# Seven half-size products in place of eight for the first layer's output projection

## The chip, the cores and the metric

The kernel runs on one core of a Trainium2 chip. TensorE (PE in the profile) multiplies matrices into PSUM banks; VectorE (DVE), ScalarE (ACT) and GpSimd (POOL) do the element-wise work; 16 DMA engines move data between HBM and the on-chip memory (SBUF). Transfers are issued from queues, here that of SyncE (SP) and, in the change, that of POOL. The metric is the device time of one execution in microseconds (us), as the median of several runs.

## The reference

A two-layer decoder trunk on 512 tokens of width 1024, in float32. The first layer is a pooling mixer, the second a latent attention; a final RMSNorm follows. What matters here is the end of the first layer and what comes next:

```python
def pool_layer(x, norm_g, w_in, w_group, scale, w_out):
    ...
    mixed = jnp.einsum('bsgc,gcd->bsgd', pooled, w_group).reshape(B, S, POOL_WIDTH) * scale
    y = mixed * jax.nn.silu(z)
    return x + y @ w_out          # y: 512 x 2048, w_out: 2048 x 1024
```

Its result is normalised (RMSNorm) and multiplied by `mla_w_in` in the second layer.

## The kernel before

Matrix products keep float32 accuracy with three products of rounded parts. Every operand is split into `hi` (rounded, by an ACT copy) and `lo` (the rest, by a DVE or POOL subtraction), and `mm3` (L181 to L184) adds hi x hi, lo x hi and hi x lo into a PSUM bank. One `mm3` is three matmuls of a 128x128 stationary tile with up to 512 moving columns. `halves` (L186 to L188) is the pair of instructions that splits a tile.

Weights come in strips. `Strip` (L129 to L168) loads pieces of at most 512 columns into five `raw` buffers over SP's queue (L154, L160) and splits them into a hi and a lo tile of 2048 columns (L166, L167). These tiles share the tag `w` with four buffers (`WB`), so two strips are in flight.

The activations `y` (2048 channels in 16 blocks of 128 partitions, times 512 tokens) lie transposed on chip. They are written group by group, four blocks per group, at L523 (`y[:, c, :]`), after the group's matmuls (L511 to L525) that read `d_hi` and `d_lo`. `h_hi` and `h_lo` (L210, L211) hold the split, normalised tokens of the first layer; their last readers are the gate products of the last group (L503 to L510), which come just before that group's matmuls.

The output projection `OutProj` (L528 to L572) accumulates over the 16 channel blocks, two to a strip, into eight PSUM banks: four tiles of 128 tokens times two halves of 512 output columns. A strip needs 2 x 4 x 2 = 16 calls of `mm3`, 48 matmuls; the eight strips make 384. For each strip four weight pieces and two `y` blocks are split. The last strip is worked off tile by tile (`last_block`, L587 to L592): two banks are finished, added to the residual `xs` (`add`, L572), and `norm_a` (L214 to L218) squares the rows on ACT, forms the reciprocal root in two small POOL steps (L202, L203) and scales on DVE (L217). `norm_b` (L220 to L227) transposes the result on TensorE and splits it into `h_hi`/`h_lo`, where the second layer's first products (`lat_block`, L608 to L636) read it. Their weight strips use the same tag `w`, and POOL makes their `lo` parts.

The order in which each engine issues its instructions, and the semaphores between engines, are fixed when the kernel is compiled, by a planner that goes by the order of the code and by when it reckons each instruction's inputs and buffers to be ready; an instruction whose inputs are ready earlier can be put ahead of one that the code has before it. At run time each engine keeps to that order.

Of the kernel before, what the change touches and what calls it, by code (L numbers as in the profile page):

```python
# [11 lines left out]
F32 = mybir.dt.float32  # L12
F32R = mybir.dt.float32r
I32 = mybir.dt.int32
AF = mybir.ActivationFunctionType
ALU = mybir.AluOpType

P = 128
D = 1024
S = 512  # L20
NT = S // P
KD = D // P
W = 2048
# [9 lines left out]
PAD = 16  # L33
SCALE = (DN + DR) ** -0.5
WB = 4
# [15 lines left out]
def trunk_kernel(  # L51
# [17 lines left out]
    nc = tc.nc  # L69
    pe, act, dve, pool = nc.tensor, nc.scalar, nc.vector, nc.gpsimd  # L70

    def f32(ap):
        return ap.bitcast(F32)
# [4 lines left out]
    wp = ctx.enter_context(tc.tile_pool(name="wp", bufs=2))  # L78
# [5 lines left out]
    def open_pool(name, stack, **kw):  # L84
        return stack.enter_context(
            tc.tile_pool(name=name, bufs=1, reuse_waits="tile", **kw)
        )
# [3 lines left out]
    wk = open_pool("wk1", phase)  # L91

    def bank(dtype=F32):
        return ps.tile([P, 512], dtype, name="bank", tag="bank")

    def xn_tile(dtype=F32, width=D):
        return nm.tile([P, width], dtype, name="xn", tag="xn", bufs=2)


    xs = cp.tile([P, NT, D], F32, name="xs")  # L100
# [9 lines left out]
    def row(src, n, name, **kw):  # L110
        t = cp.tile([P, n], F32, name=name, **kw)
        nc.sync.dma_start(t, src.partition_broadcast(P))
        return t
# [15 lines left out]
    class Strip:  # L129


        def __init__(self, parts, cuts=1, small=False):
            width, kw = (WS, dict(tag="ws", bufs=2)) if small else (W, dict(tag="w", bufs=WB))
            self.hi = wp.tile([P, width], F32R, name="w_hi", **kw)
            self.lo = wp.tile([P, width], F32R, name="w_lo", **kw)
            self.views, self.pieces, at = [], [], 0
            for src, a, c in parts:
                hi, lo = (
                    t[:, at : at + a * c].rearrange("p (a c) -> p a c", a=a)
                    for t in (self.hi, self.lo)  # L140
                )
                self.views.append((hi, lo))
                at += a * c
                w = min(c // cuts, RC)
                g = min(a, RC // w)
                if len(src.shape) == 4:
                    g = 1
                for c0 in range(0, c, w):
                    for a0 in range(0, a, g):
                        n = min(g, a - a0)  # L150
                        raw = wp.tile([P, RC], F32, name="raw", tag="raw", bufs=RB)
                        raw = raw[:, : n * w]
                        if len(src.shape) == 4:
                            nc.sync.dma_start(  # L154
                                raw.rearrange("p (m c) -> p m c", m=src.shape[2]), src[:, a0]
                            )
                            raw = raw.rearrange("p (a c) -> p a c", a=n)
                        else:
                            raw = raw.rearrange("p (a c) -> p a c", a=n)
                            nc.sync.dma_start(raw, src[:, a0 : a0 + n, c0 : c0 + w])  # L160
                        i = (slice(None), slice(a0, a0 + n), slice(c0, c0 + w))
                        self.pieces.append((raw, hi[i], lo[i]))
# [7 lines left out]
    def strip(parts, eng=dve, small=False):  # L170
        st = Strip(parts, small=small)
        st.split(st.pieces, eng)
        return st.views
# [4 lines left out]
    def w_rows(w, k0, k):  # L178
        return w[k0 * P : (k0 + k) * P, :].rearrange("(k p) c -> p k c", p=P)

    def mm3(o, a, b, start, stop):  # L181
        pe.matmul(o, a[0], b[0], start=start, stop=False)  # L182
        pe.matmul(o, a[1], b[0], start=False, stop=False)  # L183
        pe.matmul(o, a[0], b[1], start=False, stop=stop)  # L184

    def halves(src, hi, lo):  # L186
        act.activation(hi, src, AF.Copy)  # L187
        dve.tensor_tensor(lo, src, f32(hi), ALU.subtract)  # L188
# [17 lines left out]
    def inv_rms(src, junk, n):  # L206
        return rsqrt(sum_sq(src, junk, n))

    y = cp.tile([P, KW, S], F32, name="y")
    h_hi = hp.tile([P, KD, S], F32R, name="h_hi")  # L210
    h_lo = hp.tile([P, KD, S], F32R, name="h_lo")  # L211
    hp.tile([P, 24], F32, name="rim")

    def norm_a(t, g):  # L214
        xn = xn_tile()
        rs = inv_rms(xs[:, t, :], xn, D)
        dve.scalar_tensor_tensor(xn, xs[:, t, :], rs, g, ALU.mult, ALU.mult)  # L217
        return xn  # L218

    def norm_b(t, xn):  # L220
        for b in range(2):
            pt = bank()
            for i in range(4):
                k = 4 * b + i
                pe.transpose(pt[:, i * P : (i + 1) * P], xn[:, k * P : (k + 1) * P], ident)
            o = (slice(None), slice(4 * b, 4 * b + 4), slice(t * P, (t + 1) * P))
            halves(pt.rearrange("p (k c) -> p k c", k=4), h_hi[o], h_lo[o])  # L227

    def hmm(o, wv, ct, cols):
        for k in range(KD):  # L230
            a = tuple(v[:, k, ct * P : (ct + 1) * P] for v in wv)
            b = tuple(v[:, k, cols] for v in (h_hi, h_lo))
            mm3(o[:, cols], a, b, k == 0, k == KD - 1)
# [218 lines left out]
    def branch():  # L452

        u = wk.tile([P, 2, PAD + S], F32, name="u", tag="t4", bufs=4)
        pool.memset(u[:, :, :PAD], 0.0)
        return u

    d_hi = wk.tile([P, 4, S], F32R, name="d_hi")
    d_lo = wk.tile([P, 4, S], F32R, name="d_lo")
# [22 lines left out]
    for g in range(4):  # L482
        pooled_from = []
        if g == 0:
            for j in range(2):
                u = branch()
# [5 lines left out]
            g_mla = row(mla_norm[0], D, "g_mla", tag="gain")  # L492
        else:
            for j in range(2):
                (wv,) = strip([(w_cols(w_in, g * 512 + j * 256, 256), KD, 256)])
                u = branch()
                for i in range(2):
                    b = bank()
# [4 lines left out]
        for j in range(2):  # L503
            (wv,) = strip([(w_cols(w_in, W + g * 512 + j * 256, 256), KD, 256)])
            for i in range(2):
                b = bank()
                hmm(b, wv, i, whole_row)
                z = wk.tile([P, S], F32, name="zs", tag="z", bufs=8)
# [3 lines left out]
        for o in range(4):  # L512
            b = bank()
            for k in range(4):
                mm3(
                    b,
                    tuple(v[:, k, o * P : (o + 1) * P] for v in wv),
                    (d_hi[:, k, :], d_lo[:, k, :]),
                    k == 0,
                    k == 3,  # L520
                )
            c = 4 * g + o
            dve.scalar_tensor_tensor(  # L523
                y[:, c, :], b, gcol[:, GS + c : GS + c + 1], zs[o], ALU.mult, ALU.mult
            )  # L525


    class OutProj:  # L528
# [3 lines left out]
        def load(self, s, tile_of):  # L532
            (wv,) = strip([(w_rows(self.w, 2 * s, 2), 2, D)])
            ys = []
            for j in range(2):
                yh, yl = tile_of("h", j), tile_of("l", j)
                halves(y[:, 2 * s + j, :], yh, yl)
                ys.append((yh, yl))
            self.st[s] = (wv, ys)
# [7 lines left out]
        def block(self, s, t, n, j):  # L547
            wv, ys = self.st[s]
            if (t, n) not in self.acc:
                self.acc[t, n] = bank()  # L550
            mm3(
                self.acc[t, n],
                tuple(v[:, t * P : (t + 1) * P] for v in ys[j]),
                tuple(v[:, j, n * 512 : (n + 1) * 512] for v in wv),
                s == 0 and j == 0,
                j == 1 and s == (6 if self.apart == (t, n) else 7),
            )
# [13 lines left out]
            c = slice(n * 512, (n + 1) * 512)  # L571
            return dve.tensor_tensor(xs[:, t, c], self.acc[t, n], xs[:, t, c], ALU.add)  # L572

    def y_tile(half, j):
        return wk.tile([P, S], F32R, name=f"y{half}", tag="z", bufs=8)


    o1 = OutProj(pool_w_out[0])
    for s in range(8):
        o1.load(s, y_tile)  # L580
        if s < 7:
            for j in range(2):
                for t in range(NT):
                    for n in range(2):
                        o1.block(s, t, n, j)

    def last_block(t):  # L587
        for n in range(2):
            for j in range(2):
                o1.block(7, t, n, j)  # L590
            o1.add(t, n)
        return norm_a(t, g_mla)  # L592

    w_in2 = mla_w_in[0]
    xn = {t: last_block(t) for t in range(2)}
    xn[2] = last_block(2)
    norm_b(0, xn[0])
    xn[3] = last_block(3)
    norm_b(1, xn[1])

    phase.close()
    lT = ExitStack()
# [192 lines left out]
    for i in range(3, 8):  # L795
# [5 lines left out]
    wk = ap = open_pool("wk3", phase)  # L801
# [3 lines left out]
        out=mask[:, 384:],  # L805
# [179 lines left out]
    for h in range(H):  # L985
        p, odd = divmod(h, 2)
        g, t = divmod(h + 5, 4)
# [35 lines left out]
    for s in range(2, 8):  # L1023
# [4 lines left out]
    o = [  # L1028
        ap.tile([P, D], F32, name="o", tag=tag, bufs=n)
        for tag, n in (("pm", 2), ("pm", 2), ("pt_hi", 1), ("pt_lo", 1))  # L1030
    ]
# [113 lines left out]
```

## Time and profile before

| | us |
|---|---|
| median of three runs | 739.25 (738.48 to 739.72) |
| profiled execution, its time | 740.2 |
| profiled execution, its span | 738.2 |
| TensorE busy | 722.7 (98%) |
| VectorE busy | 384.8 (52%) |
| ScalarE busy | 318.9 (43%) |
| GpSimd busy | 96.9 (13%) |

The span runs from the first to the last instruction of the profiled execution; its own time also counts what lies around it. The projection's matmuls start at 234.7 us; its last sums and the norms lie between 312 and 332 us. A line such as `L182 PE MATMUL bank<-w_hi,yh` names the line of the kernel, the engine, the operation, and the tiles written and read; the releaser in brackets is what an engine had waited for before it.

### The profile page before, as it was taken

What the parts mean: (1) busy time and instruction counts of PE and PEld (TensorE: products, weight loads), DVE (VectorE), ACT (ScalarE), POOL (GpSimd) and SP (SyncE); (2) the same over time, 40 slices, a digit from 0 to 9 for tenths busy, and PEclk for the clock granted to TensorE, in tenths of its full rate; (3) what the DMA queues carried; (4) which work ended last, traced back from release to release, by engine and by line L of the source; (5) the groups of instructions that cost most, each with busy time, mean ns of one, the idle gap of its engine ahead of it and who ended that gap; (6) DMA issues with size and microseconds to landing.
All of it is one profiled execution on the core that took longest, in us unless ns stands there. A gap on an engine that the chain in (4) does not pass through costs nothing.

```text
span 738.2 us, 10030 instructions
## 1 busy us (share of the span) xinstructions
PE 722.7 (98%) x3619; PEld 616.8 (84%) x3619; DVE 384.8 (52%) x800; ACT 318.9 (43%) x727; POOL 96.9 (13%) x143
## 2 busy tenths in 40 slices
PE   7999999999999999999999999999999999999995
PEld 6988888888888888889888888898888988888884
DVE  5864454464565333271644311686876877744325
ACT  6452242232333323243652325665566565623314
POOL 5000000000000000153600005221232020000006
PEclk8999999999999999999999999999999999999998
DMA  8342332332233233124333424122132131113203
GB/s 256 106 141 64 108 115 72 100 115 86 85 115 92 80 115 107 43 78 130 95 115 98 131 76 122 51 50 79 51 96 75 31 108 58 57 58 115 83 18 114
DMA packets 61985, 68.09 MB, mean 92 GB/s; under 512 B 11760, under 2 KB 45680, under 8 KB 61936
## 3 DMA queue, kind: packets, MB, share of 16 engines
q1 hardware_dynamic: 61792, 67.26, 30.4%
q8 instruction: 28, 0.46, 0.2%
q10 hardware_dynamic: 144, 0.20, 0.1%
q14 instruction: 21, 0.17, 0.1%
HBM read 61.15 MB, written 2.10 MB: 86 GB/s over the span
## 4 chain that ended last, share of the span: by engine, by line
PE 92%; DVE 4%; ACT 1%; POOL 1%; issue 1%; DMA 0%; POOLq 0%; SPq 0%; ACTq 0%
PE bank L183 28%; PE bank L184 28%; PE bank L182 28%; PE bank L941 2%; PE bank L300 2%; PE bank L904 1%; PE bank L905 1%; DVE xn L217 1%; PE bank L907 1%; ACT pm L927 1%; DVE pm L933 1%; PE bank L270 1%; DVE nm L924 0%; DMA xs<-in_x 0%; ACT xn L197 0%
## 5 line engine op out<-in xcount | busy, mean ns | idle before, releaser
L166 ACT ACTIVATE w_hi<-raw 128x512 fp32r<-128x512 f32 (+2 forms) x240 | 127.3, 584 | 192.3 <-PE bank L183 184.7
L167 DVE TENSOR_TENSOR w_lo<-raw,w_hi 128x512 fp32r<-128x512 f32 x172 | 111.8, 690 | 172.6 <-ACT w_hi L166 172.6
L182 PE MATMUL bank<-h_hi,w_hi 128*128 128x512 f32 x368 | 143.4, 390 | 0.0
L184 PE MATMUL bank<-h_lo,w_hi 128*128 128x512 f32 x368 | 143.2, 389 | 0.0
L183 PE MATMUL bank<-h_hi,w_lo 128*128 128x512 f32 x368 | 143.2, 389 | 0.0
L167 POOL TENSOR_TENSOR w_lo<-raw,w_hi 128x256 fp32r<-128x256 f32 (+2 forms) x68 | 62.2, 945 | 304.7 <-ACT w_hi L166 304.6
L184 PEld LDWEIGHTS bank<-h_lo,w_hi 128*128 128x128 f32 x368 | 69.1, 188 | 14.4
L182 PEld LDWEIGHTS bank<-h_hi,w_hi 128*128 128x128 f32 x368 | 69.1, 188 | 14.3
L183 PEld LDWEIGHTS bank<-h_hi,w_lo 128*128 128x128 f32 x368 | 69.1, 188 | 14.2
L182 PE MATMUL bank<-w_hi,yh 128*128 128x512 f32 x128 | 49.9, 390 | 0.0
L184 PE MATMUL bank<-w_lo,yh 128*128 128x512 f32 x128 | 49.8, 389 | 0.0
L183 PE MATMUL bank<-w_hi,yl 128*128 128x512 f32 x128 | 49.8, 389 | 0.0
L182 PE MATMUL bank<-latT_hi,w_hi 128*128 128x512 f32 x104 | 42.3, 407 | 0.0
L184 PE MATMUL bank<-latT_lo,w_hi 128*128 128x512 f32 x104 | 40.7, 391 | 0.0
L183 PE MATMUL bank<-latT_hi,w_lo 128*128 128x512 f32 x104 | 40.7, 391 | 0.0
L911 DVE CUSTOM_DVE_ANT_0 pm<-bank,mask 128x128 f32<-128x128 f32 (+2 forms) x64 | 30.6, 489 | 16.0 <-PE bank L184 11.0
L927 ACT ACTIVATE pm<-pm,nm 128x128 f32<-128x128 f32 (+1 forms) x64 | 35.3, 557 | 2.4 <-DVE nm L924 2.0
L187 ACT ACTIVATE pt_hi<-bank 128x512 fp32r<-128x512 f32 (+2 forms) x48 | 20.1, 491 | 22.4 <-PE bank L941 22.4
L184 PEld LDWEIGHTS bank<-w_lo,yh 128*128 128x128 f32 x128 | 24.0, 188 | 5.0
L182 PEld LDWEIGHTS bank<-w_hi,yh 128*128 128x128 f32 x128 | 24.0, 188 | 5.0
L183 PEld LDWEIGHTS bank<-w_hi,yl 128*128 128x128 f32 x128 | 24.0, 188 | 4.9
L184 PE MATMUL bank<-d_lo,w_hi 128*128 128x512 f32 x64 | 25.3, 395 | 0.0
(204 smaller groups left out, 1385.4 us busy)
## 6 DMA issues: line engine op xcount, KB each, us to landing
raw<-in_pool_w_in SPq DMA_DIRECT2D x64, 256.0 KB, 3.0
raw<-in_pool_w_out SPq DMA_DIRECT2D x32, 256.0 KB, 3.5
raw<-in_mla_w_in SPq DMA_DIRECT2D x32, 256.0 KB, 3.1
raw<-in_mla_w_out SPq DMA_DIRECT2D x32, 256.0 KB, 3.4
raw<-in_mla_w_q_b SPq DMA_DIRECT2D x36, 128.0 KB, 2.4
raw<-in_pool_w_group SPq DMA_DIRECT2D x16, 256.0 KB, 2.6
q_r<-stack SPq DMA_DIRECT2D x64, 64.0 KB, 2.0
raw<-in_mla_w_kv_b SPq DMA_DIRECT2D x16, 256.0 KB, 3.0
```

What stands on the lines that cost most here:

```text
L166: act.activation(hi, raw, AF.Copy)
L167: ins = eng.tensor_tensor(lo, raw, f32(hi), ALU.subtract)
L182: pe.matmul(o, a[0], b[0], start=start, stop=False)
L183: pe.matmul(o, a[1], b[0], start=False, stop=False)
L184: pe.matmul(o, a[0], b[1], start=False, stop=stop)
L187: act.activation(hi, src, AF.Copy)
L217: dve.scalar_tensor_tensor(xn, xs[:, t, :], rs, g, ALU.mult, ALU.mult)
L270: pe.transpose(pts[t // 2][k % 4][:, c : c + P], xn[t][:, k * P : (k + 1) * P], ident)
L300: pe.matmul(first[i][:, c], w0.views[0][a][:, k, i * P : (i + 1) * P], (h_hi, h_lo)[b][:, k, c], start=k == 0 and n == 0, stop=k == KD - 1 ...
L911: dve.tensor_tensor_reduce(out=pm[:, OFF[i] : OFF[i] + w], in0=o[:, :w], in1=mask[:, S - w :], scale=1.0, scalar=-3.0e38, op0=ALU.add, op1 ...
L927: act.activation(v, v, AF.Exp, bias=nm[:, i : i + 1], scale=SCALE, accum_out=l[:, i : i + 1])
L941: pe.transpose(b[:, n : n + P], pm[:, OFF[i] + j * P : OFF[i] + (j + 1) * P], ident)
```

## The change

The projection is computed by Strassen's scheme in the form with running sums. The token axis is cut in two (256 each), the channel axis in two (1024 each), the output columns in two (LEFT and RIGHT, 512 each). With `a` for quarters of y (first index tokens, second channels) and B for quarters of w_out (first index channels, second columns), the seven products are

| product | tokens | weights | bank set | added to the residual of |
|---|---|---|---|---|
| 1 | a11 | B11 | acc | tokens 1 LEFT (+) |
| 2 | s = a21 - a22 | B11+B12 | both | tokens 2 RIGHT (+) |
| 3 | s - a11 | B11+B12+B22 | acc, on top of 1 | tokens 1 RIGHT (-) |
| 4 | s - a11 + a12 | B22 | both, on top of 2 | tokens 1 RIGHT (+) |
| 5 | a11 - a21 | B22+B12 | acc, on top of 1 and 3 | tokens 2 RIGHT (-) |
| 6 | a12 | B21 | last | tokens 1 LEFT (+) |
| 7 | a22 | B11+B12+B22+B21 | acc, on top of 1, 3 and 5 | tokens 2 LEFT (+) |

A product is two tiles of 128 tokens times eight channel blocks times one `mm3`, 48 matmuls with 512 columns. The bank sets are two banks each. After most products a bank is added to the residual in SBUF (`gather`) while it stays in PSUM for the next product on top.

The weight sums are formed in memory: `x_sum` and `y_sum` are four tiles each (128 x 2 x 512, 2.1 MB in all) on buffers that the pooling no longer uses. A plain load from SP's queue brings the first quarter; further quarters are added to it by transfers issued from POOL's queue with an accumulate operation, four per quarter, 512 KB each. `halves_of` splits a tile in pieces of 1024 columns on ACT and DVE. Token sums are DVE additions of 512 columns; token splits go to one half (slot) of the columns of `h_hi`/`h_lo`, the slots alternating. The norm of tokens 0 to 255 is issued before product 7 is.

```diff
-    def mm3(o, a, b, start, stop):
...
+    def mm3(o, a, b, start, stop, more=False):
...
-    o1 = OutProj(pool_w_out[0])
-    for s in range(8):
-        o1.load(s, y_tile)
-        if s < 7:
...
-    xn = {t: last_block(t) for t in range(2)}
-    xn[2] = last_block(2)
-    norm_b(0, xn[0])
-    xn[3] = last_block(3)
-    norm_b(1, xn[1])
...
+        def load(self, half, c, add=False):
+            for i, t in enumerate(self.tiles):
+                src = w_rows(w_out, half * 8 + 2 * i, 2)[:, :, c]
+                if add:
+                    pool.dma_start(t, src, accum_op=ALU.add)
+                else:
+                    nc.sync.dma_start(t, src)
...
+    def halves_of(raws, eng=dve):
+
+        out = []
+        for i in range(2):
+            hi = wp.tile([P, W], F32R, name="w_hi", tag="w", bufs=WB)
+            lo = wp.tile([P, W], F32R, name="w_lo", tag="w", bufs=WB)
+            hv, lv = (t.rearrange("p (k c) -> p k c", k=4) for t in (hi, lo))
             for j in range(2):
...
+                k = slice(2 * j, 2 * j + 2)
+                act.activation(hv[:, k, :], raws[2 * i + j], AF.Copy)
+                eng.tensor_tensor(lv[:, k, :], raws[2 * i + j], f32(hv[:, k, :]), ALU.subtract)
+            out.append((hv, lv))
+        return out
...
+    def multiply(banks, strips, slot, start, then=None):
+        def one(q, t):
+            c = slice(slot * 256 + t * P, slot * 256 + (t + 1) * P)
+            for k in range(4):
+                mm3(
...
+        for q in range(2):
+            for t in range(2):
+                one(q, t)
+                if then and q == 1:
+                    then(t)
...
+    x_sum = Summed(
+        [wk.tile([P, 2, PAD + S], F32, name="b_x", tag="t4", bufs=4)[:, :, :S] for _ in range(4)]
+    )
+    y_tiles = [wk.tile([P, 4, S], F32, name="b_y", tag=n) for n in ("d_hi", "d_lo")]
+    y_sum = Summed([t[:, 2 * i : 2 * i + 2, :] for t in y_tiles for i in range(2)])
+    s1, s3 = sums("s1"), sums("s3")
+
+    acc = [bank() for _ in range(2)]
+    x_sum.load(0, LEFT)
+    split_tokens(a11, 1)
+    multiply(acc, x_sum.strips(), 1, True)
+    x_sum.load(0, RIGHT, add=True)
+    combine(s1, a21, a22, ALU.subtract)
+    for t in range(2):
+        gather(t, LEFT, acc[t])
+    both = [bank() for _ in range(2)]
+    split_tokens(s1, 0)
+    multiply(both, x_sum.strips(), 0, True)
+    y_sum.load(1, RIGHT)
+    x_sum.load(1, RIGHT, add=True)
...
+    multiply(acc, x_sum.strips(), 1, False)
+    x_sum.load(1, LEFT, add=True)
...
+    multiply(both, y_sum.strips(), 0, False)
+    y_sum.load(0, RIGHT, add=True)
...
+    multiply(acc, y_sum.strips(), 1, False)
...
+    multiply(last, columns_of(1, LEFT), 0, True)
+    xn = {}
+    for t in range(2):
+        gather(t, LEFT, last[t])
+        xn[t] = norm_a(t, g_mla)
+    split_tokens(a22, 1)
+    norm_b(0, xn[0])
+
+    def token_tile(t):
+        gather(2 + t, LEFT, acc[t])
+        xn[2 + t] = norm_a(2 + t, g_mla)
+        if t == 0:
+            norm_b(1, xn[1])
+
+    multiply(acc, x_sum.strips(), 1, False, token_tile)
```

More of the change, by code (lines that the diff above doesn't have):

```diff
@@ L179, in w_rows @@
         return w[k0 * P : (k0 + k) * P, :].rearrange("(k p) c -> p k c", p=P)
-    def mm3(o, a, b, start, stop):
-        pe.matmul(o, a[0], b[0], start=start, stop=False)
-        pe.matmul(o, a[1], b[0], start=False, stop=False)
-        pe.matmul(o, a[0], b[1], start=False, stop=stop)
+    def mm3(o, a, b, start, stop, more=False):
+        pe.matmul(o, a[0], b[0], start=start, stop=False, skip_group_check=more)
+        pe.matmul(o, a[1], b[0], start=False, stop=False, skip_group_check=more)
+        pe.matmul(o, a[0], b[1], start=False, stop=stop, skip_group_check=more)
     def halves(src, hi, lo):
@@ L572, in add @@
             return dve.tensor_tensor(xs[:, t, c], self.acc[t, n], xs[:, t, c], ALU.add)
-    def y_tile(half, j):
-        return wk.tile([P, S], F32R, name=f"y{half}", tag="z", bufs=8)
-    o1 = OutProj(pool_w_out[0])
-    for s in range(8):
-        o1.load(s, y_tile)
-        if s < 7:
-            for j in range(2):
[L583 to L592, printed above, removed]
@@ L594, in trunk_kernel, with __init__, strips @@
-    w_in2 = mla_w_in[0]
-    xn = {t: last_block(t) for t in range(2)}
-    xn[2] = last_block(2)
-    norm_b(0, xn[0])
-    xn[3] = last_block(3)
-    norm_b(1, xn[1])
+    w_out = pool_w_out[0]
+    LEFT, RIGHT = slice(0, 512), slice(512, D)
+    class Summed:
+        def __init__(self, tiles):
+            self.tiles = tiles
+        def load(self, half, c, add=False):
[5 more added lines that the diff above has]
+                    nc.sync.dma_start(t, src)
+        def strips(self):
+            return halves_of(self.tiles)
@@ new lines, in columns_of, with quarter, sums @@
+    def columns_of(half, c):
+        return [
+            strip([(w_rows(w_out, half * 8 + 4 * i, 4)[:, :, c], 4, 512)])[0] for i in range(2)
+        ]
+    def quarter(t, half):
+        return [y[:, half * 8 + 2 * i : half * 8 + 2 * i + 2, t * 256 : (t + 1) * 256] for i in range(4)]
+    a11, a12, a21, a22 = (quarter(t, h) for t in range(2) for h in range(2))
+    def sums(name):
+        return [
+            wk.tile([P, 2, 256], F32, name=name, tag="z", bufs=8) for _ in range(4)
+        ]
@@ new lines, in combine, with split_tokens @@
+    def combine(out, a, b, op):
+        for o, u, v in zip(out, a, b):
+            dve.tensor_tensor(o, u, v, op)
+    def split_tokens(src, slot):
+        c = slice(slot * 256, (slot + 1) * 256)
+        for i, v in enumerate(src):
+            halves(v, h_hi[:, 2 * i : 2 * i + 2, c], h_lo[:, 2 * i : 2 * i + 2, c])
+    def multiply(banks, strips, slot, start, then=None):
[3 more added lines that the diff above has]
+                mm3(
+                    banks[t],
+                    tuple(v[:, 4 * q + k, c] for v in (h_hi, h_lo)),
+                    tuple(v[:, k, :] for v in strips[q]),
+                    start and q == 0 and k == 0,
+                    q == 1 and k == 3,
+                    more=not start,
+                )
[4 more added lines that the diff above has]
+                    then(t)
@@ new lines, in gather @@
+    def gather(t, c, b, op=ALU.add):
+        dve.tensor_tensor(xs[:, t, c], xs[:, t, c], b, op)
+    x_sum = Summed(
+        [wk.tile([P, 2, PAD + S], F32, name="b_x", tag="t4", bufs=4)[:, :, :S] for _ in range(4)]
+    )
+    y_tiles = [wk.tile([P, 4, S], F32, name="b_y", tag=n) for n in ("d_hi", "d_lo")]
[4 more added lines that the diff above has]
+    split_tokens(a11, 1)
@@ new lines, in trunk_kernel @@
+    multiply(acc, x_sum.strips(), 1, True)
[9 more added lines that the diff above has]
+    for t in range(2):
+        gather(2 + t, RIGHT, both[t])
+    combine(s1, s1, a11, ALU.subtract)
+    split_tokens(s1, 1)
+    multiply(acc, x_sum.strips(), 1, False)
@@ new lines, in trunk_kernel @@
+    x_sum.load(1, LEFT, add=True)
+    for t in range(2):
+        gather(t, RIGHT, acc[t], ALU.subtract)
+    combine(s1, s1, a12, ALU.add)
+    split_tokens(s1, 0)
+    multiply(both, y_sum.strips(), 0, False)
+    y_sum.load(0, RIGHT, add=True)
+    for t in range(2):
+        gather(t, RIGHT, both[t])
+    combine(s3, a11, a21, ALU.subtract)
+    split_tokens(s3, 1)
+    multiply(acc, y_sum.strips(), 1, False)
+    for t in range(2):
+        gather(2 + t, RIGHT, acc[t], ALU.subtract)
+    last = [bank() for _ in range(2)]
@@ L601, in trunk_kernel @@
+    split_tokens(a12, 0)
+    multiply(last, columns_of(1, LEFT), 0, True)
+    xn = {}
+    for t in range(2):
+        gather(t, LEFT, last[t])
[8 more added lines that the diff above has]
+    multiply(acc, x_sum.strips(), 1, False, token_tile)
+    w_in2 = mla_w_in[0]
     phase.close()
```

## The prediction

> **What bounds the kernel now.** I read the page first, then the stage that is changed by stretches of time, then who waits in it.
>
> ```profile
> span 738.2 us, 10030 instructions
> PE 722.7 (98%) x3619; PEld 616.8 (84%) x3619; DVE 384.8 (52%) x800; ACT 318.9 (43%) x727; POOL 96.9 (13%) x143
> PE 92%; DVE 4%; ACT 1%; POOL 1%; issue 1%; DMA 0%; POOLq 0%; SPq 0%; ACTq 0%
> ```
>
> TensorE is busy 98% of the span and holds 92% of the chain that ended last. A matmul less is therefore a gain, and any hole torn into TensorE is a loss of its own length. The stage that is changed begins at 234.7 us. In the view by stretches:
>
> ```profile
> core 0: us, PE busy (x) PEld busy (x) DVE busy (x) ACT busy (x) POOL busy (x), PEclk, DMA share, GB/s
> 9.00:12.00 3.00, 2.41 (x10) 2.07 (x10) 2.23 (x6) 1.49 (x5) 1.91 (x4) 0.50 1.02 376
> 235.00:312.00 77.00, 77.00 (x342) 63.73 (x341) 26.52 (x42) 23.14 (x43) 0.41 (x1) 1.00 0.29 91
> 312.00:330.00 18.00, 16.79 (x93) 14.48 (x92) 12.00 (x15) 9.78 (x20) 10.54 (x16) 1.00 0.23 63
> ```
>
> From 235 to 312 us all 342 matmuls have 512 columns and nothing interrupts them: 77.0 / 342 = 0.225 us each, at clock 1.00. DVE has 26.5 of 77 us, ACT 23.1, and the DMA engines are 29% used. So the stage has spare room on every other unit, which is what the change spends. Its end (312 to 330 us) holds 1.2 us of TensorE idleness.
>
> **What the change removes.** Eight strips of 48 matmuls become seven products of 48: 48 x 0.225 = **10.8 us less** on TensorE. A product lasts 10.8 us, each half of it (four of its eight k-blocks) 5.4 us. Stationary and moving shapes stay 128x128 and 128x512, so I keep 0.225 us. This term is an upper limit: nothing else in the edit shortens TensorE's work.
>
> **What it adds: the handover of the weight buffers.** The four buffers of tag "w" hold two hi/lo pairs, and one product now needs both. A pair is free again when its half product is done, so the split for the same half of the next product has the 5.4 us of the other half.
>
> ```profile
> ACT w_hi L166 <- PE bank L183: 184.7, 47, 8.5
> 211.24 1.06 ACT L187 ACTIVATE d_hi<-sums 128x1024 fp32r<-128x1024 f32 x1 [3.09 <-DVE sums L479]
> 212.33 1.23 DVE L188 TENSOR_TENSOR d_lo<-sums,d_hi 128x1024 fp32r<-128x1024 f32 x1 [1.13 <-ACT d_hi L187]
> 245.78 2.20 ACT L166 ACTIVATE w_hi<-raw 128x512 fp32r<-128x512 f32 x4 [4.86 <-PE bank L183]
> 246.44 2.50 DVE L167 TENSOR_TENSOR w_lo<-raw,w_hi 128x512 fp32r<-128x512 f32 x4 [4.80 <-ACT w_hi L166]
> ```
>
> The first row says that this wait for a free buffer is already what ACT's copies wait for, 47 times. A 128x1024 piece costs 1.06 us on ACT and 1.23 on DVE, so the first matmul of a half can go 1.06 + 1.23 = 2.3 us after its tiles are there, and the pair is split after 1.06 + 2 x 1.23 = 3.5 us. Against 5.4 us that leaves 3.1 us to spare. Cost: nothing, covered by the other half's matmuls; without that cover it would be 2.3 us per half.
>
> **The accumulating transfers** decide the case. Each of the four sums (for products 2, 3, 5 and 7) adds 2.1 MB from HBM into tiles that already hold data. A tile's add can start only after ACT and DVE have split its old content, and must land 2.3 us before the half product that uses it. No transfer of this kind stands in the trace, so the price has to be bounded.
>
> ```profile
> q1 hardware_dynamic: 497, 1.13, 102.0%
> raw<-in_pool_w_out SPq DMA_DIRECT2D x32, 256.0 KB, 3.5
> xs<-in_x SPq DMA_DIRECT2D x2, 512.0 KB, 6.9
> q_r<-stack SPq DMA_DIRECT2D x64, 64.0 KB, 2.0
> L160 SPq DMA_DIRECT2D raw<-in_pool_w_out x12: 327/328/347, 259.8 to 291.8; - x12
> ```
>
> From 9 to 12 us the 16 engines were full (102%) and moved 376 GB/s of plain loads. One pair of tiles, 1.05 MB, takes 2.8 us at that rate: the lower bound s = 2.8 us, if an add moves like a plain load. An add has two operands to fetch and one result to write; if both fetches take turns, s = 5.6; if both fetches and the write follow one another, s = 8.4, the upper bound. I take **s = 6.0**: two fetches, and part of the two issues per pair, which cost 0.33 us each on SP's queue. After the bytes I add 2.0 us to landing, what the smallest transfers (64 KB) take.
>
> Product 1 itself finds all ready: x_sum's tiles are last read at 213.56 (212.33 + 1.23 above), 21 us ahead, its tokens are y's first half. With product 1 starting at 0, the plain load of y_sum holds the engines until 5.6 us (its tiles are d_hi and d_lo, read until 0). Then seven pairs follow one another: the second of product 2, two of product 3, two of product 7 (their issue is ready before product 5's, and POOL's queue keeps order), two of product 5. The last lands at 5.6 + 7s + 2.0 and is due 2.3 us before the second half of product 5, at 48.6 - 2.3 = 46.3 us. All lateness together is thus 7s - 38.7 us: **+3.3 us** at s = 6.0, spread over products 3 and 5 with no single hole above 1.8 us; nothing up to s = 5.5; +20.1 at 8.4. Late next is everything behind the split in ACT's and DVE's order, token splits included.
>
> The Trainium skill has a rule against this change: "Collectives: The Full Stack", section "The bandwidth ceiling", says that an add in the DMA path runs at about half the rate of a copy because it needs two source reads. By it alone an estimate of 5.6 us per pair gives 0.5 us of lateness; no run here shows it yet.
>
> **DVE and ACT.** The rows give 0.62 us for a 512-wide subtraction in a batch (2.50 / 4), 0.69 for an addition out of PSUM:
>
> ```profile
> 312.59 0.69 DVE L572 TENSOR_TENSOR xs<-bank,xs 128x512 f32<-128x512 f32 x1 [8.70 <-PE bank L184]
> 218.43 0.60 ACT L509 ACTIVATE zs<-bank 128x512 f32<-128x512 f32 x1 [2.94 <-PE bank L184]
> 223.69 0.63 ACT L166 ACTIVATE w_hi<-raw 128x512 fp32r<-128x512 f32 x1 [4.67 <-PE bank L183]
> 224.23 0.58 ACT L509 ACTIVATE zs<-bank 128x512 f32<-128x512 f32 x1
> ```
>
> DVE: 24 weight pieces x 1.2 + 8 x 0.62 + 28 token splits x 0.62 + 16 token sums x 0.62 + 14 gathers x 0.69 = 28.8 + 5.0 + 17.4 + 9.9 + 9.7 = 70.8 us, some 8 of it before product 1, in seven products of 75.6 us. In product 2 it is tightest: 4.8 + 1.4 + 2.5 + 2.5 = 11.2 us of work in 10.8, unless the sum for product 3 went ahead. ACT: 24 x 1.06 + 36 x 0.55 = 45 us, no bound. Engines work in the order fixed at compile time, and the last rows show that this order runs ahead of the text: the first strip of w_out is copied at 223.69, before a SiLU (224.23) that the code has earlier. So a gather that waits for a product need not stand ahead of the next split. I price what does go wrong at **+2.0 us**, a third of a microsecond at six handovers, nearer to the zero that today's handovers show (77.0 of 77.0) than to the other bound: 2.5 us (four token splits) ahead of the weight split in each of five products, 12.5.
>
> **The end of the stage.** Before and after, the second-layer norm of the last tokens follows the last matmuls.
>
> ```profile
> 311.59 3.67 POOL L167 TENSOR_TENSOR w_lo<-raw,w_hi 128x352 fp32r<-128x352 f32 x4 [114.27 <-ACT w_hi L166]
> 315.92 0.22 POOL L202 TENSOR_SCALAR rs<-ssq 128x1 f32<-128x1 f32 x1 [0.66 <-ACT xn L197]
> 314.68 1.06 ACT L197 ACTIVATE xn<-xs 128x1024 f32<-128x1024 f32 x1 [2.01 <-DVE xs L572]
> 316.83 1.29 DVE L217 SCALAR_TENSOR_TENSOR xn<-xs,rs,g_mla 128x1024 f32<-128x1024 f32 x1 [0.82 <-POOL rs L203]
> 326.99 1.09 PE L225 MATMUL bank<-ident,xn 128*128 128x128 f32 x8 [1.21 <-DVE xn L217]
> ```
>
> Today's hole is the 1.21 us of the last row. After the change tokens 0 to 255 are normalised under product 7, a gain of up to 1.2 us; but the first latent strip gets its buffers only 5.4 us before the end instead of a whole strip ahead, and its 3.67 us on POOL can stand ahead of the norm's small POOL steps, a loss of up to 3.7. I take **+0.5 us**. SP's queue issues 16 larger plain loads (8 of 512 KB, 8 of 256 KB) for 32 and is emptier; its wait for d_hi at 0 holds back only loads for buffers that are full. POOL's queue has no other work until the latent strip.
>
> **The sum**, against the profiled execution's 740.2 us (span 738.2): -10.8 + 3.3 + 2.0 + 0.5 = -5.0, so 735.2. That execution stands 0.95 above the median of the runs, 739.25; a median of **734.2 us** follows.
>
> **The rivals.**
> - *The adds are hidden* (s up to 5.5): the lateness is nothing and the handovers run like today's or little worse: 740.2 - 10.8 + 0 to 2.5 - 0.95 = 728.5 to 731. For it: 29% DMA use today. Against it: seven pairs and y_sum's load fill 5.6 + 7 x 5.6 = 44.8 of 46.3 us even when only two fetches count.
> - *The adds become the bound; slower.* Place: the wait of the weight split for its tile, at products 2, 3 and 5. It decides from 7s - 38.7 = 8.3, s = 6.7 us per pair (157 GB/s). At s = 8.0: 17.3 us late, 739.25 - 10.8 + 17.3 + 2.5 = 748.2. For it: each microsecond of s counts seven times, and the 8.4 of three passes lies beyond it. Against it: fetch and write work on both ends at once in the plain loads at 376 GB/s. A hole of 7.8 us (product 5) would also lower the clock: the 9 to 12 us row shows 0.50 granted after TensorE had waited at the start. "TensorE: Matmul & The Clock Gate", section "What's actually happening", in the Trainium skill, puts that threshold at one idle window of about 3.4 us, by which the forecast's holes, under 2 us, stay at full clock; the row agrees in direction, and none here shows the threshold.
> - *DVE becomes the bound*: the 12.5 us bound above in place of 2.0, adds as forecast: 739.25 - 10.8 + 3.3 + 12.5 + 0.5 = 744.8; half of it gives 738.5. For it: 11.2 us of work in product 2. Against it: only that product is so full.
> - *Fewer matmuls than thought are saved*: a row count of 336 in place of 384 settles it; nothing in the code speaks for another number, so it gets no chance of its own.
>
> **How the numbers follow.** The forecast with s from 5.6 to 6.4 gets 0.36, adds hidden 0.20, adds as bound 0.32, DVE as bound 0.12. A change of 0.2% (1.5 us) is about what a measurement of this kernel tells from none. Faster: 0.33 + 0.20 + 0.04 of DVE's half-way case = 0.57; same: 0.03 + 0.03 = 0.06; slower: 0.31 + 0.06 = 0.37. The range runs from 728 (nothing late) to 750 (s a little above 8), leaving out the last part to s = 8.4. The forecast's own range is 731 to 738.
>
> **What would show it.** 336 matmuls at 0.225 us in the stage. An accumulating transfer queue whose pairs take about 6 us at full use. Waits of w_hi's copies: on TensorE when the adds are hidden, on the DMA into b_x or b_y when they are late, with TensorE's holes at the starts of products 3 and 5; product 2 free of them. Holes without such a DMA wait, with DVE busy, would be the third rival. I am wrong if a pair takes over 6.7 us, or if POOL needs longer to issue an add than the engines need to move it.

## The result, and the profile after

The changed kernel takes **728.19 us** (median, 727.47 to 728.39), the kernel before 739.36 us in the same comparison: ratio 0.9849, 95% interval 0.9832 to 0.9866. In a later comparison the same pair gave 727.48 and 739.60 (0.9838, 0.9824 to 0.9851). The gain is 11.2 to 12.1 us; the forecast was 5.0. The page and the view by stretches of the changed kernel (columns as before):

```profile
span 726.6 us, 9988 instructions
PE 712.1 (98%) x3571; PEld 607.1 (84%) x3571; DVE 417.6 (57%) x834; ACT 337.0 (46%) x739; POOL 116.9 (16%) x159
PE 86%; DMA 4%; issue 3%; DVE 3%; POOL 2%; ACT 1%; SPq 0%; POOLq 0%; ACTq 0%
```

```profile
234.00:245.00 11.00, 11.00 (x50) 9.08 (x49) 10.72 (x15) 6.33 (x8) 4.85 (x4) 1.00 1.00 258
245.00:256.00 11.00, 11.00 (x50) 9.13 (x49) 8.48 (x12) 6.13 (x8) 2.59 (x3) 1.00 1.13 206
256.00:267.00 11.00, 11.00 (x51) 9.09 (x50) 11.00 (x15) 6.77 (x10) 6.53 (x6) 1.00 1.06 185
267.00:278.00 11.00, 11.00 (x50) 9.13 (x49) 6.20 (x8) 4.29 (x6) 3.06 (x3) 1.00 1.04 184
278.00:289.00 11.00, 10.60 (x47) 8.41 (x46) 10.02 (x14) 8.17 (x13) 0.00 (x0) 1.00 0.35 74
300.00:311.00 11.00, 10.41 (x55) 8.52 (x54) 7.33 (x8) 6.10 (x11) 5.50 (x8) 1.00 0.07 18
```

Each of the first five stretches is about one product. TensorE is busy without a break in products 1 to 4, while the DMA engines are full (share 1.00 and above) and DVE has up to 11.00 of 11 us. The change has used up most of the room that the stage had: the DMA engines are full over four products, and DVE is full in one stretch (256 to 267 us) with 2.5 to 4.8 us left in two others. What TensorE waits for in the whole stage and its end:

```profile
PE bank L226 <- DVE xn L218: 0.6, 1, 0.6
PE bank L185 <- DVE w_lo L608: 0.4, 1, 0.4
```

TensorE's matmuls fell from 3619 to 3571, by the 48. The span fell by 11.6 us: 10.9 for them (48 x 0.227); 0.8 back at product 5, which takes 11.64 us (277.64 to 289.28) where the others take 10.88, because of the 0.41 us hole and slower matmuls around it; 0.6 gained at the end, where the hole before the norm's transposes is 0.6 in place of 1.2. Another 0.7 us lie ahead of the change, and 0.2 are not accounted for: the 0.7 are there because the same 1057 matmul records end at 234.0 in place of 234.7 us, with less waiting at the kernel's start, which the edit does not touch.

```profile
0.00:234.70 234.70, 230.05 (x1057) 192.29 (x1058) 127.40 (x215) 88.61 (x160) 11.00 (x31) 0.99 0.36 112
```

```profile
0.00:234.00 234.00, 230.23 (x1057) 192.05 (x1058) 133.83 (x223) 90.45 (x161) 13.85 (x33) 0.99 0.40 120
```

(The first row is the kernel before, the second the changed one.) How fast the adds move is seen where ACT starts to copy a tile as soon as it has landed, in the timeline of the changed kernel:

```profile
246.57 1.06 ACT L607 ACTIVATE w_hi<-b_x 128x1024 fp32r<-128x1024 f32 x1 [2.10 <-DMA b_x<-in_pool_w_out]
249.05 1.06 ACT L607 ACTIVATE w_hi<-b_x 128x1024 fp32r<-128x1024 f32 x1 [1.42 <-DMA b_x<-in_pool_w_out]
256.78 1.06 ACT L607 ACTIVATE w_hi<-b_x 128x1024 fp32r<-128x1024 f32 x1 [0.58 <-DMA b_x<-in_pool_w_out]
259.22 1.06 ACT L607 ACTIVATE w_hi<-b_x 128x1024 fp32r<-128x1024 f32 x1 [1.38 <-DMA b_x<-in_pool_w_out]
274.01 1.06 ACT L607 ACTIVATE w_hi<-b_y 128x1024 fp32r<-128x1024 f32 x1 [2.34 <-DMA b_y<-in_pool_w_out]
277.66 1.06 ACT L607 ACTIVATE w_hi<-b_y 128x1024 fp32r<-128x1024 f32 x1 [2.59 <-DMA b_y<-in_pool_w_out]
```

At their fastest, tiles follow one another by 2.48 and 2.44 us, 5.0 us a pair (1.05 MB, 212 GB/s). The train as a whole is slower: from the copy at 249.05 to that at 277.66 lie five pairs, 28.6 / 5 = **5.7 us** a pair, where the prediction took 6.0. The stretches from 245 to 278 us say the same: 206, 185 and 184 GB/s with the engines full. The last interval shown, 3.65 us, is the longest, and the one hole follows it. Product 1 starts at 234.10, product 5 at 277.64, when the later tile of its first pair had only just landed (copied at 277.66, above):

```profile
234.10 0.39 PE L183 MATMUL bank<-w_hi,h_hi 128*128 128x512 f32 x1
277.64 0.39 PE L183 MATMUL bank<-w_hi,h_hi 128*128 128x512 f32 x1
278.76 1.23 DVE L608 TENSOR_TENSOR w_lo<-b_y,w_hi 128x1024 fp32r<-128x1024 f32 x1 [2.43 <-ACT w_hi L607]
280.04 0.50 PE L185 MATMUL bank<-w_lo,h_hi 128*128 128x512 f32 x1 [0.41 <-DVE w_lo L608]
```

### The profile page after: what moved, and what is told of

The parts are those of the page before. It is cut to its first block, busy times and chain, and to the rows that moved or that the text cites. A ratio compares the mean times of both kernels' runs of the same rounds, so it can differ in the third digit from the quotient of the medians.

```text
span 726.6 us, 9988 instructions
## 1 busy us (share of the span) xinstructions
PE 712.1 (98%) x3571; PEld 607.1 (84%) x3571; DVE 417.6 (57%) x834; ACT 337.0 (46%) x739; POOL 116.9 (16%) x159
## 3 DMA queue, kind: packets, MB, share of 16 engines
q0 software_dynamic: 4352, 8.39, 6.6%
## 4 chain that ended last, share of the span: by engine, by line
PE 86%; DMA 4%; issue 3%; DVE 3%; POOL 2%; ACT 1%; SPq 0%; POOLq 0%; ACTq 0%
PE bank L185 26%; PE bank L183 26%; PE bank L184 26%; PE bank L1059 2%; PE bank L301 2%; DMA b_y<-in_pool_w_out 2%; PE bank L1022 1%; PE bank L1023 1%; DMA b_x<-in_pool_w_out 1%; POOL b_x L591 1%; DMA raw<-in_pool_w_in 1%; PE bank L1025 1%; PE bank L226 1%; ACT pm L1045 1%; DVE pm L1051 1%
## 5 line engine op out<-in xcount | busy, mean ns | idle before, releaser
L166 ACT ACTIVATE w_hi<-raw 128x512 fp32r<-128x512 f32 (+2 forms) x216 | 114.1, 580 | 153.3 <-PE bank L184 142.3
L167 DVE TENSOR_TENSOR w_lo<-raw,w_hi 128x512 fp32r<-128x512 f32 x148 | 96.8, 690 | 135.6 <-ACT w_hi L166 135.6
L185 PE MATMUL bank<-w_lo,h_hi 128*128 128x512 f32 (+1 forms) x176 | 64.2, 365 | 0.4 <-DVE w_lo L608 0.4
L183 PE MATMUL bank<-w_hi,h_hi 128*128 128x512 f32 (+1 forms) x176 | 64.6, 367 | 0.0
L184 PE MATMUL bank<-w_hi,h_lo 128*128 128x512 f32 (+1 forms) x176 | 64.1, 364 | 0.0
L185 PEld LDWEIGHTS bank<-w_lo,h_hi 128*128 128x128 f32 x176 | 33.0, 188 | 5.3 <-DVE w_lo L608 0.8
L183 PEld LDWEIGHTS bank<-w_hi,h_hi 128*128 128x128 f32 x176 | 33.0, 188 | 4.4
L184 PEld LDWEIGHTS bank<-w_hi,h_lo 128*128 128x128 f32 x176 | 33.1, 188 | 4.3
```

Of the source, the lines that this page charges most:

```text
L166: act.activation(hi, raw, AF.Copy)
L167: ins = eng.tensor_tensor(lo, raw, f32(hi), ALU.subtract)
L183: pe.matmul(o, a[0], b[0], start=start, stop=False, skip_group_check=more)
L184: pe.matmul(o, a[1], b[0], start=False, stop=False, skip_group_check=more)
L185: pe.matmul(o, a[0], b[1], start=False, stop=stop, skip_group_check=more)
```

## The experiments

All are edits of the changed kernel. A time without a range is that of one execution; executions of one kernel lie up to 1.7 us apart. The theory after reading its trace was that the adds are just hidden, in the main because their due time is later than predicted (a half product first reads the later tile of its pair six matmuls after its start) and because DVE's order runs ahead; the rivals were slack in the adds' own rate and DVE as the true limit.

**The price of adding.** The transfers overwrite instead of adding.

```diff
-                    pool.dma_start(t, src, accum_op=ALU.add)
+                    pool.dma_start(t, src)
```

> Leaves out the adding: the 16 transfers from POOL's queue overwrite the tile instead of adding to it, so the weight sums are not formed; all instructions, waits and orders stay. Theory (an add fetches twice, 6.0 us per pair of tiles in the changed kernel's queue row, and just fits under the products): a pair drops to some 3 us of queue time, the DMA engines are no longer full from 234 to 278 us, TensorE's 0.40 us hole there goes, and the time falls by 0.4 us, to about 727.8. Rival (adds move like plain loads, and the queue's 6.0 us comes from elsewhere, such as POOL's issue of 1.2 us each): the pair stays at 6 us and the engines stay full.

727.20 us (726.77 to 728.42), ratio to the kernel before 0.9845 (0.9829 to 0.9862): no difference from the changed kernel that its interval shows. The hole at product 5 is gone; that alone shows little, since it is also below the view's limit in a second profile of the changed kernel (last run below). The queue's row, first of the changed kernel, then of this one, and this one's stretch with full engines:

```profile
q0 software_dynamic: 4352, 8.39, 6.6%
```

```profile
q0 software_dynamic: 2304, 8.39, 3.5%
237.00:244.00 7.00, 7.00 (x33) 5.79 (x32) 7.00 (x11) 3.79 (x5) 2.81 (x4) 1.00 1.02 366
```

The same 8.39 MB take 6.6% of the engines' span with adding, 3.5% without (6.0 and 3.2 us a pair): per byte an add takes 1.9 times a load. The rates agree: plain loads fill the engines at 366 GB/s, adds at 184 to 206 in the stretches and at 212 at their fastest, so an add costs 1.7 to 2.0 loads. The expectation's 0.4 us is too small for this measurement to tell; that the adds nearly double the engines' work, and that the engines have room without them, is shown.

**The due time.** Each half product goes through the later tile first.

```diff
-            for k in range(4):
+            for k in (2, 3, 0, 1):
...
-                    start and q == 0 and k == 0,
-                    q == 1 and k == 3,
+                    start and q == 0 and k == 2,
+                    q == 1 and k == 1,
```

> Same products, but each half product goes through its second tile's two channel blocks before the first tile's, so the half can start only when the later tile of its pair has landed and is split. That is the due time that the prediction used. Theory (the prediction's due time was too early because the later tile is needed only six matmuls, 1.36 us, into the half): holes come back at products 2, 3 and 5, 1.5 to 4 us in all against 0.4, time 729.5 to 732. Rival (the due time did not matter, the adds landed earlier than worked out): holes stay at 0.4 to 0.8 us.

727.47 us, and no hole at all in the seven products. So the holes that the theory expected did not come. But the tiles came earlier too, and the due time was hardly put to the test:

```profile
272.71 1.06 ACT L607 ACTIVATE w_hi<-b_y 128x1024 fp32r<-128x1024 f32 x1 [1.17 <-DMA b_y<-in_pool_w_out]
275.17 1.06 ACT L607 ACTIVATE w_hi<-b_y 128x1024 fp32r<-128x1024 f32 x1 [1.40 <-DMA b_y<-in_pool_w_out]
```

Product 5's first pair was copied at 272.71 and 275.17; product 1 starts at 233.97 here, so the later tile came 41.2 us after it, in the changed kernel 277.66 - 234.10 = 43.6 us. Product 5 starts 43.5 us after product 1 in both, and by the prediction's due time, 2.3 us before it, 41.2 is just in time and 43.6 is some 2.3 us late. The changed kernel's hole was only 0.41 us. The due time therefore did matter in the changed kernel: TensorE reads the later tile's `w_lo` first with the product's ninth matmul, 8 x 0.227 = 1.8 us after its start. Why the tiles came earlier here isn't shown. In the runs whose edits leave the adds alone the later tile came 39.9 to 43.2 us after product 1's start, so whether this edit or the execution did it is open.

**More to add.** Product 7's adds are issued twice.

```diff
     x_sum.load(1, LEFT, add=True)
+    x_sum.load(1, LEFT, add=True)
```

> The four adds for product 7 are issued twice, so product 7's weights hold one quarter twice; two more pairs stand ahead of product 5's adds. Theory (the adds fill the engines, with well under 2 us of slack, and each further pair is paid for in full): two pairs x 6.0 us = 12 us more queue, less at most 2 us of slack, less the last tile that falls behind product 5's first: TensorE holes of 8 to 12 us at product 5, time 736 to 740. Rival (the tiles have much slack, since the 0.4 us hole is all that was seen): 0 to 4 us.

739.72 us, 11.5 us more. Its timelines of TensorE and POOL, and two stretches:

```profile
284.11 0.80 PE L183 MATMUL bank<-w_hi,h_hi 128*128 128x512 f32 x1 [7.42 <-ACT w_hi L607]
289.24 0.80 PE L183 MATMUL bank<-w_hi,h_hi 128*128 128x512 f32 x1 [1.80 <-ACT w_hi L607]
```

```profile
274.41 1.20 POOL L591 DMA_DIRECT2D b_x<-in_pool_w_out  x1 [7.60 <-DMA b_x<-in_pool_w_out]
```

```profile
284.00:287.00 3.00, 2.85 (x6) 1.67 (x6) 1.22 (x1) 0.06 (x1) 0.00 (x0) 0.50 1.10 195
294.00:296.00 2.00, 2.00 (x10) 1.63 (x10) 1.65 (x2) 2.00 (x5) 0.00 (x0) 1.00 0.00 0
```

TensorE stands still for 7.42 + 1.80 = 9.2 us at product 5, and some 3 us more are lost to a clock of 0.50 behind the holes. That is the predicted slower rival, called up by hand: its place and kind were right, and the adds' slack is far below the 11 us of two pairs. How far can't be read off: a tile's second add had to wait for its first to land (POOL idle 7.60 us), which holds up product 5's adds beyond the bytes.

**More work for DVE.** All token sums are done twice; then, in a run of its own, only those of product 3.

```diff
         for o, u, v in zip(out, a, b):
             dve.tensor_tensor(o, u, v, op)
+        for o, u, v in zip(out, a, b):
+            dve.tensor_tensor(o, o, v, op)
```

> Each of the 16 token sums is followed by a second one of the same kind, so the sums are not the reference's; DVE gets 16 x 0.62 = 10 us more, some 7 of it in products 1 to 4, whose DVE share is already 8.5 to 11.0 of 11 us. Theory (DVE had 2 to 5 us to spare in products 2, 4, 5 and 6, and its order runs ahead): holes of 0 to 2 us, time 728 to 730. Rival (DVE was on the edge): 2.5 us in each of products 2 to 4, time 733 to 736.

738.26 us: over 10 us slower, far more than either expectation. TensorE's waits in its timeline:

```profile
269.88 0.50 PE L185 MATMUL bank<-w_lo,h_hi 128*128 128x512 f32 x1 [1.85 <-DVE w_lo L608]
281.65 0.49 PE L183 MATMUL bank<-w_hi,h_hi 128*128 128x512 f32 x1 [1.05 <-ACT h_hi L188]
286.35 0.79 PE L185 MATMUL bank<-w_lo,h_hi 128*128 128x512 f32 x1 [3.01 <-DVE w_lo L608]
```

The holes sum to 6.1 us with one of 0.23; the rest is again a lower clock behind the last one, not behind the first, as two stretches show:

```profile
270.00:272.00 2.00, 2.00 (x9) 1.66 (x10) 2.00 (x3) 0.00 (x0) 1.64 (x2) 1.00 0.03 4
288.00:290.00 2.00, 2.00 (x6) 1.52 (x6) 2.00 (x3) 0.00 (x0) 0.00 (x0) 0.50 0.00 0
```

So DVE, or the order in which it works (each doubled sum also depends on the first), is near its limit too. How near:

```diff
     combine(s1, s1, a11, ALU.subtract)
+    combine(s1, s1, a11, ALU.subtract)
```

> Only the token sums of product 3 (s - a11, four instructions) are done twice, 2.5 us more for DVE, so that product's sum is wrong. Theory after the doubling of all sums cost 10 us (DVE has some 2 to 3 us to spare over products 1 to 3, and every microsecond beyond stops TensorE): no hole or one under 1 us, time 727 to 728.5. Rival (the dependence of each further sum on the one before, not DVE's time, cost the 10 us): 2.5 us or more, time 729.5 to 731.

727.83 us with one hole of 0.2 us:

```profile
PE bank L185 <- DVE w_lo L608: 0.2, 1, 0.2
```

2.5 us more are absorbed at product 3, with the same kind of dependence; 10 over all sums are not. The other way round, DVE is relieved of some 4 us:

```diff
+        n = 16 if out is a else 256
         for o, u, v in zip(out, a, b):
-            dve.tensor_tensor(o, u, v, op)
+            dve.tensor_tensor(o[:, :, :n], u[:, :, :n], v[:, :, :n], op)
```

> The token sums of products 3 and 4 cover 16 of 256 columns each (the rest keeps its old content, so these sums are not formed); DVE is relieved of about 8 x 0.5 = 4 us. Theory (DVE does not hold TensorE up in the changed kernel): no gain, 727 to 728. Rival (DVE's order costs the changed kernel something that its holes do not show): over 1.5 us faster.

727.28 us: nothing gained. In the changed kernel DVE, although busy 11.00 of 11 us in one stretch, does not hold TensorE up.

**The adds against DVE sums.** One part of the change undone: the quarters come by plain loads, and DVE adds them.

```diff
-                    pool.dma_start(t, src, accum_op=ALU.add)
+                    for k in range(2):
+                        raw = wp.tile([P, RC], F32, name="raw", tag="raw", bufs=RB)
+                        nc.sync.dma_start(raw, src[:, k, :])
+                        dve.tensor_tensor(t[:, k, :], t[:, k, :], raw, ALU.add)
```

> The weight sums are made by DVE: every further quarter comes by plain loads from SP's queue in pieces of 512 columns into the raw buffers, and DVE adds each piece into its tile; everything else as in the changed kernel. DVE gets 32 x 0.62 = 20 us more, 91 us in all against 76 us of products. Theory (DVE becomes the bound where the sums are made, products 2 to 5): 8 to 16 us slower than the changed kernel, 736 to 744, so that the seven products alone would bring little. Rival (DVE's order leaves enough room, work slides to products 6 and 7): 0 to 4 us slower, 728 to 732.

744.40 us (744.26 to 745.44), slower even than the kernel before: ratio 1.0069 (1.0052 to 1.0086). Three of TensorE's five waits, and stretches around the first:

```profile
260.15 0.50 PE L185 MATMUL bank<-w_lo,h_hi 128*128 128x512 f32 x1 [2.58 <-DVE w_lo L611]
276.99 0.50 PE L185 MATMUL bank<-w_lo,h_hi 128*128 128x512 f32 x1 [2.21 <-DVE w_lo L611]
291.12 0.81 PE L184 MATMUL bank<-w_hi,h_lo 128*128 128x512 f32 x2 [1.79 <-DVE h_lo L189]
```

```profile
262.00:264.00 2.00, 2.00 (x7) 1.52 (x6) 2.00 (x3) 0.00 (x0) 0.00 (x0) 0.50 0.00 0
266.00:268.00 2.00, 2.00 (x10) 1.68 (x9) 1.72 (x3) 1.52 (x2) 0.00 (x0) 1.00 0.81 251
```

The five waits sum to 10.2 us, all for halves that DVE makes, and most of the rest is half clock behind them. DVE was busy 62.7 of 66 us from 234 to 300 us and waited only 1.6 us for the quarters to land, so it is DVE's work, not the plain loads, that holds TensorE up. With 20 us of sums on DVE, the seven products are worth less than nothing. The gain belongs to both halves of the change together.

**Product 5's adds ahead of product 7's, and the later tile needed later.** Three runs: the first edit, the second, and both.

```diff
-    x_sum.load(1, LEFT, add=True)
...
-    y_sum.load(0, RIGHT, add=True)
+    seen = y_sum.load(0, RIGHT, add=True)
+    with tc.issue_after(seen.ins):
+        x_sum.load(1, LEFT, add=True)
```

```diff
         for q in range(2):
-            for t in range(2):
-                one(q, t)
+            for ks in ((0, 1), (2, 3)) if not then else (range(4),):
+                for t in range(2):
+                    one(q, t, ks)
```

> The adds for product 7 are issued after those for product 5. Theory (product 5's adds were behind the two pairs of product 7, landing 9.0 and 11.6 us after their issue): product 5's tiles land some 4 us earlier, limited then by their own issue after product 4's split, TensorE's 0.40 us hole at product 5 goes, product 7's tiles still have 15 us; time 727.8. Rival (something else made the hole): it stays.

> Each half product of products 1 to 6 does the first tile's two channel blocks for both token tiles before the second tile's, so the second tile is needed 12 matmuls (2.72 us) into the half instead of 6 (1.36 us). Theory (due time by tile): the hole at product 5 goes, 0.4 us less, time 727.8. Rival: unchanged at 0.4 us.

> Both edits together: product 5's adds before product 7's, and the second tile needed 12 matmuls into the half. Theory: no hole in products 1 to 6, 727.8 us, no difference from the changed kernel that a measurement can tell (0.05%). Rival (the orders cost more than the trace's holes show): over 1 us either way.

727.21 and 726.81 us, and with both edits 727.23 (0.9837, 0.9823 to 0.9852), none with a hole in the seven products. With the first edit, this stretch shows what the order frees:

```profile
256.00:267.00 11.00, 11.00 (x50) 9.13 (x49) 11.00 (x16) 6.83 (x9) 2.44 (x2) 1.00 0.19 28
```

The engines are at 0.19 there in place of 1.06; product 7's adds run later. Both edits, and the changed kernel, once more on one chip:

> The changed kernel as it is, beside the next one on the same chip: 727.5 to 728.5, and holes of 0 to 0.5 us at product 5, since the hole in its first profile came after a stretch in which the adds moved 90 GB/s in place of some 205.

> Product 5's adds before product 7's, and the second tile needed 12 matmuls into the half, as before. Theory: the adds of the changed kernel land late only in some executions, so this gains 0 to 1 us over it: 727 to 727.5. Rival: no difference.

The changed kernel gives 727.48 us (0.9838, 0.9824 to 0.9851), with both edits 726.99 (0.9827, 0.9814 to 0.9841). The intervals overlap: a gain of half a microsecond is not shown. This time the view counts no wait of the changed kernel in the seven products, but its product 5 still takes 11.19 us in place of 10.88 (the later tile was copied 43.2 us after product 1's start), where with both edits it takes 10.88. So the delay at product 5 belongs to the changed kernel and varies with the execution, 0.8 and 0.3 us in its two profiles.

## Why the prediction was wrong

The forecast, -5.0 us, was the 10.8 us of the matmuls less three losses that came small or not at all. The time is that of its first rival, "the adds are hidden" (728.5 to 731), a little below its lower edge, but not by the mechanism that the rival gave: it asked for 5.5 us a pair or less, and the train of adds took 5.7.

1. *48 matmuls less at 0.225 us.* Right: 48 records fewer, TensorE's busy time 10.6 us shorter.
2. *Weight buffers handed over at no cost.* Right: no wait of TensorE in products 1 to 4.
3. *The accumulating transfers, +3.3 us.* This is the step that failed first. The forecast was made of a landing time and a due time, and both were off.

The due time: the formula wants both tiles of a pair 2.3 us before their half product. For product 5's first pair it has the landing at 5.6 + 6 x 6.0 + 2.0 = 43.6 us after product 1's start, 2.7 us late. The later tile was copied at 43.6 (43.2 in the second profile), but TensorE waited 0.41 us and lost 0.8 (0.3 in the second profile), because it needs that tile's `w_lo` only 1.8 us into the half. That the landing agrees is in part luck: a pair took 5.7 us and not 6.0, but the second pair of product 2 was copied at 15.0 us and not 13.6.

The landing: product 5's last tile was copied at 48.5 us (47.8 in the second profile), not at 5.6 + 7 x 6.0 + 2.0 = 49.6. Against the formula's due time of 46.3 it is still 2.2 us late (1.5). So of the 3.3 us of lateness that were forecast, 1.1 went (1.8) because the tiles came earlier, 1.4 (1.2) because they were needed later, and 0.8 (0.3) came. In three runs with edits elsewhere the first pair's later tile came 2.4 to 3.7 us earlier, and nothing was lost. No run changes the due time alone with the tiles as late as in this profile, so these shares are read from the traces.

The order of the transfers, the full engines and the place of the delay were as told. POOL's issue (1.2 us for an add, in the view of the adds' line of the changed kernel below) runs beside the bytes.

```profile
L591 POOL DMA_DIRECT2D b_x<-in_pool_w_out x12: 1194/1206/1524, 226.8 to 262.2; - x12
```

4. *The Trainium skill's rule.* "Collectives: The Full Stack", section "The bandwidth ceiling", gives a reduction about half the rate of a copy because the add needs two source reads, for the rings of a collective. The traces agree for a local add: 184 to 212 against 366 GB/s, 0.50 to 0.58 of it. The estimate of 5.6 us a pair that the prediction worked out by this rule is close to the 5.7 measured; the 0.5 us of lateness that the prediction drew from it is near the 0.8 and 0.3 measured by luck, as it goes by the same early due time.
5. *Handovers on DVE and ACT, +2.0 us.* Measured nothing: but for the delay at product 5, which begins with a late landing, DVE and ACT cost TensorE no time. The amount of work was right (DVE up to 11.00 of 11 us), though the fullest stretch is that of product 3 and not of product 2, which has 8.48. That the compile-time order put the sums where they fit is the likely reason; no run tests it. The rival "DVE becomes the bound" was close by all the same: 2.5 us more are absorbed, 10 us more cost over 10, and 20 us more turn the gain into a loss.
6. *The end of the stage, +0.5 us.* Measured -0.6: the hole before the norm's transposes fell from 1.2 to 0.6 us, half of what was given as the most to be gained. POOL's latent strip (314.28 to 318.15 us) did stand ahead of the last tokens' norm step, at 318.23, but TensorE had other matmuls and was busy 18.00 of 18 us from 312 to 330.
7. *The clock.* I wrote that holes under 2 us stay at full clock by the Trainium skill's threshold of one idle window of 3.4 us ("TensorE: Matmul & The Clock Gate", "What's actually happening"). The changed kernel's hole was too short to try it. In the runs with holes one stop of 1.85 us agrees (no drop after it at 269.88 in the doubled sums). But in the run with DVE sums a stop of 1.79 us, ended at 291.12, was followed by a clock of 0.50, and so was the one of 2.58 us, both shorter than the rule's window; the measurement decides. So holes of about 2 us can already cost more than their length, and times worked out from holes alone are too low.

The range, 728 to 750, holds the measured 728.19 at its very edge, and the second measurement, 727.48, lies outside. With s uncertain and counted seven times, the forecast was a value between two outcomes (hidden or bound).

## What to carry to other kernels

Where TensorE is the bound and the other units have room, arithmetic that trades matmuls for sums can pay in full, as it did here, if each sum goes to the unit that still has room: here the weight sums to the DMA path, the token sums to DVE. Before such a change, work out each unit's load for the stage alone and how many times the uncertain price enters: here seven times. Work out with the same care which instruction first needs each tile, because 1.8 us of due time were worth as much here as the error in the landing. Afterwards the stage has little room: two pairs more to add, or 10 us more on DVE, cost the whole gain.

## What the runs showed of the hardware that was not expected

- An accumulating transfer from HBM into SBUF moved 184 to 206 GB/s over stretches with full engines and 212 GB/s at its fastest (a pair of 1.05 MB in 5.0 us); plain loads, from both queues, moved 366 GB/s in the run that leaves out the adding.
- A stop of TensorE of 2.58 us was followed by about 3 us at half clock (262 to 264 us at 0.50, back at 1.00 from 266 us, in the run with DVE sums). The length of a stop alone does not decide: 1.85 us left the clock at 1.00 in the run with doubled sums, and 1.79 us in the run with DVE sums did not. In the traces of these two runs the changes of the granted clock lie whole multiples of 3.41 us apart. In the stretches between such marks that hold the two stops (to a tenth of a us), TensorE was busy 1.82 of 3.50 us and 1.61 of 3.40 us, first the doubled sums, then the DVE sums with the stretch behind:

```profile
268.20:271.70 3.50, 1.82 (x8) 1.52 (x9) 3.50 (x5) 1.69 (x2) 1.34 (x2) 1.00 0.52 94
```

```profile
288.20:291.60 3.40, 1.61 (x7) 0.89 (x6) 3.40 (x7) 2.82 (x6) 0.00 (x0) 1.00 0.36 132
291.70:291.90 0.20, 0.20 (x1) 0.00 (x0) 0.20 (x1) 0.20 (x1) 0.00 (x0) 0.50 0.00 0
```

The stops of 2.58 and 2.21 us in the run with DVE sums, before drops, left 0.82 and 1.19 us busy in such a stretch; that of 1.53 us, with no drop, left 1.97. That the busy share of such a stretch decides fits these five stops; no run sets out to test it.
